# A two-block transformer kernel: convolution tables loaded instead of built, a home of its own for one tile, and another start

## The chip, the cores and the metric

The kernel runs on one core of one Trainium2 chip. The metric is the device time of one launch in microseconds (us), as the median of several runs. Beside it there is one profiled execution, with the start and duration of the instructions of each engine: TensorE (PE, matrix products; PEld is its weight load), VectorE (DVE), ScalarE (ACT), GpSimd (POOL) and SyncE (SP, which here issues nearly all transfers). Transfers are issued by an engine into its queue and then carried out by 16 DMA engines.

## The reference

The input is x of 256 tokens by 1024 features. Two hybrid layers (attention beside retention, then an MLP), an "even" mixer (block attention beside a pooling) and an "odd" mixer follow each other. Nearly everything is a product with streamed float32 weights. The change touches the beginning and the odd mixer, whose second half is a causal depthwise convolution with 31 taps:

```python
def odd_mixer(h, w_in, lam_re, lam_im, log_dt, b_re, b_im, c_re, c_im, d,
              glu_w, glu_b, dw, ln_g, ln_b, pw, w_out):
    z = h @ w_in
    su, gc, ca, cb, gd = jnp.split(z, ..., axis=-1)
    y = s5_ssm(su, lam_re, lam_im, log_dt, b_re, b_im, c_re, c_im, d)
    ya, yb = jnp.split(y @ glu_w + glu_b, 2, axis=-1)
    ssm_out = ya * jax.nn.sigmoid(yb) * jax.nn.silu(gc)
    conv_out = conformer_conv(ca, cb, dw, ln_g, ln_b, pw) * jax.nn.silu(gd)
    return jnp.concatenate([ssm_out, conv_out], axis=-1) @ w_out

def conformer_conv(a, gl, dw, ln_g, ln_b, pw):
    g = a * jax.nn.sigmoid(gl)
    c = lax.conv_general_dilated(g, kern, (1,), [(CONV_K - 1, 0)], feature_group_count=CONV_WIDTH)
    n = layer_norm(c) * ln_g + ln_b
    return jax.nn.silu(n) @ pw
```

s5_ssm is a diagonal state space recurrence over the 256 tokens.

## The kernel before

**Weights.** They come in chunks of 128 x 2048 float32 (1 MB, tile `raw`, three buffers), issued by SP in the order of use (`fetch`, L325; the first two chunks in four pieces of 128 x 512 each, L334). ACT rounds each chunk to `hi` (L336), DVE takes the rest `lo` (L337), each in halves with five buffers. PE makes three products of each pair of tiles: hi by the rounded activations, lo by them, and hi by the activations' rest (L404 to L406 in the first group `ng`, L391 to L393 in narrow ones).

**Order.** A framework of tiles and pools orders each engine's instructions by priorities when the program is built. A tile takes the place of an earlier one with the same pool and tag, once that one's last reader is done. On an engine, and in its queue, things go strictly in their order: an instruction that waits holds all behind it.

**Start.** SP issues the first piece of weights, then 8 KB of norm weights (`pv`), then the first pair of slices of x (128 x 2 x 256, 256 KB), and so on by turns; x is loaded in four such pairs (L1534). ACT scales and rounds x to `xs` (L464), DVE makes the rest (L465), and the first group of 48 products (`ng`, eight slices of 1024 features, six products each) begins.

**Odd mixer.** The projections come in the order su, cb, ca, cb, ca, gc, gd (banks `su`, `cb`, `ca`, `og`). For the convolution, the gated signal `g` (a part of the tile `big`, four groups of 128 channels) is copied by DMA into strips that hold four shifted copies: `strip(p)` issues 16 small transfers on SP (L1331) for two of the four groups, into `g4[p]`. Strip 0 lies in the place "pwc" (freed by ACT's last activation for `Q`, L1207, which follows POOL's memset of Q), strip 1 in the place "E", a table that DVE's `states(q)` reads for the last time in `wall<-wall,E` of states(3). `convolve(p)` makes 64 products of 128 x 32 weights `taps` (L1349; each float32 product is two records in the trace); POOL builds the taps from the packed filter in `pv` and small unit matrices in `ct`, into three buffers (L1338). Then PE makes `ys`, the S5 output, with `K` (L1403) and `Q` with the states `wall` (L1410), the layer mean `mu` over the convolution's result (L1390), the gated unit `gb` and `ga` and the output `yo`.

The line that matters most for the order is the place of the strips:

```python
g4[p] = s5["pool"].tile([P, 2, 4, GS + 1], F32, name="g4", tag=("pwc", "E")[p], bufs=1)
```

Of the kernel before, what the change touches and what calls it, by code (L numbers as in the profile page):

```python
# [45 lines left out]
LOWS, LOWW, LOWX = 1500, 250, 300  # L46
KP = 8
# [105 lines left out]
def pack_weights(cs, inp):  # L153
# [3 lines left out]
    for blocks, n in zip(cs, w):  # L157
# [17 lines left out]
       ("glub", 8), ("dw", 16 * KP), ("lng", 4), ("lnb", 4), ("sinks", 16)]  # L175
# [9 lines left out]
def strips(dw):  # L185

    t = np.zeros((4 * KP, 512), np.float32)
    t[:CONVK] = dw
    return t.reshape(4, KP, 4, 4, 32).transpose(0, 4, 2, 1, 3).reshape(P, 16 * KP)


def pack_vectors(inp):
    def v(a):
        return np.asarray(a, np.float32).reshape(-1, P).T

    cols = [v(inp["g_mix"]), v(inp["g_mlp"]), v(inp["g_final"]), v(inp["pre_norm_g_2"]), v(inp["post_norm_g_2"]),
            v(inp["e_pool_scale_2"]), v(inp["o_d_2"]), v(inp["o_glu_b_2"]),
            strips(inp["o_dw_2"][0]),
            v(inp["o_ln_g_2"]), v(inp["o_ln_b_2"]),
            np.broadcast_to(inp["sinks"].reshape(1, 16), (P, 16))]  # L200
    return np.ascontiguousarray(np.concatenate(cols, axis=1))
# [16 lines left out]
_CT = [("ident", 128), ("mask0", 128), ("maske", 256), ("ecos", 64), ("esin", 64), ("blk", 128), ("icnt", 64), ("e32", 32)]  # L218
# [11 lines left out]
def tables():  # L230
# [43 lines left out]
    put("e32", np.tile(np.eye(32), (4, 1)))  # L274
# [6 lines left out]
def build(ctx, tc, w, xin, pv_in, ct_in, s5_in, pg_in, out, parts=(0, 1, "e", "o"), dbg=None):  # L281
# [33 lines left out]
    def fetch(pieces=None):  # L315
# [10 lines left out]
        for h in range(0, n, HW):  # L326
# [4 lines left out]
            for c in range(0, m, step):  # L331
# [4 lines left out]
                A.copy(hi[:, s], raw[:, rs])  # L336
# [16 lines left out]
    ones = const.tile([P, P], F32, name="ones")  # L353
    V.memset(ones, 1.0)
# [256 lines left out]
    def layer(l, xh, xl, norm, after_mixer, done):  # L611
# [218 lines left out]
        after_mixer()  # L830

# [55 lines left out]
        cur = up_out(bs[0])  # L887
        for j in range(16):
# [371 lines left out]
    def odd(pool, xh, xl, n, s5, tabs5):  # L1260
# [29 lines left out]
        pg = pool.tile([P, D], F32, name="pg", tag="cd", bufs=1)  # L1290

        def states(q):
# [5 lines left out]
            tb = pool.tile([P, 2, 4 * NC], F32, name="tb", tag="tb", bufs=2)  # L1298
# [10 lines left out]
            tb = pool.tile([P, 2, 4 * NC], F32, name="tb", tag="tb", bufs=2)  # L1309
# [24 lines left out]
        def taps(q, h):  # L1334
            n = 2 * KP
            o = PVO["dw"] + (2 * q + h) * n
            tap[q, h] = pool.tile([P, n, 32], F32, name="taps", tag="taps", bufs=3)
            G.tensor_tensor(tap[q, h], pv[:, o:o + n, None].to_broadcast([P, n, 32]),  # L1338
                            C("e32")[:, None, :].to_broadcast([P, n, 32]), op=M)

        def convolve(p):
            b = bank("sm", "cq").rearrange("p (j t) -> p j t", j=2)
            for j in range(2):
                q = 2 * p + j
                for k in range(KP):
                    if k % 4 == 0:
                        taps(q, k // 4)
                    for r in range(4):
                        T.matmul(b[32 * r:32 * r + 32, j, :], tap[q, k // 4][:, 4 * (k % 4) + r, :],  # L1349
                                 g4[p][:, j, r, k:k + S], start=k == 0, stop=k == KP - 1)  # L1350
            A.copy(cv[:, 2 * p:2 * p + 2, :], b)

        for p in range(2):
# [9 lines left out]
            if p == 0:  # L1363
# [58 lines left out]
        for p, b in enumerate(t_quad("acc", "gb", ih, il)):  # L1422
            for j in range(2):
# [3 lines left out]
                stt(gc[:, n, :], th, 1.0, gc[:, n, :], AD, M)  # L1427
        gas = t_quad("acc", "ga", ih, il, hook=lambda: later.append(nv.rstd()))
# [113 lines left out]
    nc.sync.dma_start(pv[:, NG:], pv_in[:, NG:])  # L1542
# [5 lines left out]
    gg = const.tile([P, KT], F32, name="gg")  # L1548
# [114 lines left out]
```

## Time and profile before

| | |
|---|---|
| median of three runs | 1066.11 us (1065.13 to 1067.0) |
| profiled execution, its own time | 1064.91 us |
| its span, first to last instruction | 1063.1 us |
| PE busy | 1025.0 us, 96% |
| DVE, ACT, POOL busy | 759.9, 547.1, 22.7 us |
| longest idle time of PE | 17.82 us, at 972.62 |
| PE idle before its first product | 7.37 us |

The profiled execution took 1.81 us more than its span, and lies 1.20 us under the median. "Busy" of PE counts a product until its modelled end, at whichever clock it ran, so that a busy PE can still be a slow one: the first products follow each other at 0.43 us, later ones of the same form at 0.23 us.

### The profile page before, as it was taken

The numbers are of one execution on the slowest core, as the hardware profiler recorded it, in microseconds if no ns is written. First come the engines' busy times: TensorE is split into PE (matmuls) and PEld (weight loads), VectorE is DVE, ScalarE is ACT, GpSimd is POOL, SyncE is SP. The second block draws the span as 40 slices with busy tenths as digits, with TensorE's granted clock in tenths as the row PEclk, the third lists the DMA queues.
The fourth block names the chain that finished last, engine by engine and source line by source line (L and its number), as shares of the span: only waits on it lengthen the run. The fifth ranks groups of instructions, "written<-read, shape, count | busy, mean of one in ns | idle before, by whom it ended". The sixth has DMA issues, their size and how long they took to land.

```text
span 1063.1 us, 16059 instructions
## 1 busy us (share of the span) xinstructions
PE 1025.0 (96%) x6404; PEld 882.6 (83%) x6404; DVE 759.9 (71%) x1306; ACT 547.1 (51%) x844; POOL 22.7 (2%) x24
## 2 busy tenths in 40 slices
PE   7999999999999999999999999999999998995796
PEld 5887888988888888887888988888878998994595
DVE  6768656785666659478566999965677886879085
ACT  6545653554445455547544554445475557562052
POOL 0000000000000000000000000000000030012000
PEclk9999999999999999999999999999999999998799
DMA  9654445455555545544445555555545443444121
GB/s 333 227 175 154 159 138 180 163 195 196 181 198 176 198 171 186 198 158 153 153 149 193 171 194 198 176 199 179 198 153 182 151 159 121 150 139 176 35 80 40
DMA packets 29274, 179.05 MB, mean 168 GB/s; under 512 B 3600, under 2 KB 5776, under 8 KB 8592
## 3 DMA queue, kind: packets, MB, share of 16 engines
q1 hardware_dynamic: 28624, 176.44, 48.2%
q8 instruction: 50, 0.82, 0.3%
q0 software_dynamic: 288, 1.07, 0.3%
q10 hardware_dynamic: 288, 0.52, 0.1%
q14 instruction: 24, 0.20, 0.1%
HBM read 174.82 MB, written 1.05 MB: 165 GB/s over the span
## 4 chain that ended last, share of the span: by engine, by line
PE 91%; DVE 4%; ACT 2%; DMA 1%; issue 1%; SPq 1%; DVEq 0%; ACTq 0%
PE up L842 11%; PE ng L406 6%; PE ng L404 6%; PE ng L405 6%; PE up L843 6%; PE dn L865 5%; PE dn L864 5%; PE dn L866 5%; PE gate L404 3%; PE gate L406 3%; PE gate L405 3%; PE yb L406 1%; PE yb L404 1%; PE yb L405 1%; DVE lo L337 1%
## 5 line engine op out<-in xcount | busy, mean ns | idle before, releaser
L337 DVE TENSOR_TENSOR lo<-raw,hi 128x1024 fp32r<-128x1024 f32 (+1 forms) x331 | 399.1, 1210 | 188.8 <-ACT hi L336 187.2
L336 ACT CAST hi<-raw 128x1024 fp32r<-128x1024 f32 (+1 forms) x331 | 342.6, 1039 | 313.1 <-PE dn L866 81.7
L842 PE MATMUL up<-xs,hi 128*128 128x512 f32 x512 | 182.0, 398 | 0.8 <-DVE xs L465 0.8
L843 PE MATMUL up<-xs,lo 128*128 128x256 f32 x512 | 143.6, 280 | 0.0
L842 PEld LDWEIGHTS up<-xs,hi 128*128 128x128 f32 x512 | 96.2, 188 | 24.4 <-DVE xs L465 1.2
L404 PE MATMUL ng<-hi,xs 128*128 128x512 f32 x272 | 108.4, 399 | 8.2 <-ACT xs L464 8.2
L405 PE MATMUL ng<-lo,xs 128*128 128x512 f32 x272 | 107.0, 393 | 0.0
L406 PE MATMUL ng<-hi,xs 128*128 128x512 f32 x272 | 106.7, 394 | 0.1
L864 PE MATMUL dn<-hi,uph 128*128 128x512 f32 x256 | 100.1, 391 | 0.0
L865 PE MATMUL dn<-lo,uph 128*128 128x512 f32 x256 | 99.9, 390 | 0.0
L866 PE MATMUL dn<-hi,upl 128*128 128x512 f32 x256 | 99.6, 389 | 0.0
L843 PEld LDWEIGHTS up<-xs,lo 128*128 128x128 f32 x512 | 96.7, 189 | 1.0
L404 PEld LDWEIGHTS ng<-hi,xs 128*128 128x128 f32 x272 | 51.6, 190 | 18.9 <-ACT xs L464 8.7
L406 PEld LDWEIGHTS ng<-hi,xs 128*128 128x128 f32 x272 | 51.3, 189 | 11.8 <-DVE xs L465 1.0
L405 PEld LDWEIGHTS ng<-lo,xs 128*128 128x128 f32 x272 | 51.7, 190 | 10.6
L864 PEld LDWEIGHTS dn<-hi,uph 128*128 128x128 f32 x256 | 48.1, 188 | 10.5
L866 PEld LDWEIGHTS dn<-hi,upl 128*128 128x128 f32 x256 | 48.1, 188 | 10.2
L865 PEld LDWEIGHTS dn<-lo,uph 128*128 128x128 f32 x256 | 48.1, 188 | 8.9
L404 PE MATMUL gate<-hi,xs 128*128 128x512 f32 x128 | 51.6, 403 | 0.0
L406 PE MATMUL gate<-hi,xs 128*128 128x512 f32 x128 | 49.9, 390 | 0.0
L405 PE MATMUL gate<-lo,xs 128*128 128x512 f32 x128 | 49.9, 390 | 0.0
L850 ACT COPY upa<-up 128x256 f32<-128x256 f32 x64 | 23.7, 370 | 47.8 <-PE up L843 47.8
(382 smaller groups left out, 1920.5 us busy)
## 6 DMA issues: line engine op xcount, KB each, us to landing
raw<-w_dram SPq DMA_DIRECT2D x161, 1024.0 KB, 4.9
raw<-w_dram SPq DMA_DIRECT2D x9, 256.0 KB, 5.6
g<-big SPq DMA_DIRECT2D x32, 65.8 KB, 2.0
x<-x_dram SPq DMA_DIRECT2D x4, 256.0 KB, 5.7
ctm<-ct_dram SPq DMA_DIRECT2D x1, 640.0 KB, 10.1
sp<-s_dram POOLq DMA_DIRECT2D x1, 536.0 KB, 4.0
pg<-pg_dram POOLq DMA_DIRECT2D x1, 512.0 KB, 3.7
out_dram<-xn SPq DMA_DIRECT2D x2, 256.0 KB, 2.0
```

Of the source, the lines that this page charges most:

```text
L336: A.copy(hi[:, s], raw[:, rs])
L337: V.tensor_tensor(lo[:, s], raw[:, rs], hi[:, s].bitcast(F32), op=OP.subtract)
L404: T.matmul(b[t], xh[:, k, ts], hi[:, ws], start=f, stop=False)
L405: T.matmul(b[t], xh[:, k, ts], lo[:, ws], start=False, stop=False)
L406: T.matmul(b[t], xl[:, k, ts], hi[:, ws], start=False, stop=e)
L842: T.matmul(bs[i], hi[:, ws], xs2[:, k], start=k == 0, stop=False, skip_group_check=True)
L843: T.matmul(bs[i][:, 1, :], lo[:, ws], xh2[:, k, :], start=False, stop=k == KT - 1, skip_group_check=True)
L850: A.copy(u[:, j, :], b[:, 0, :])
L864: T.matmul(accs[t][h], th[:, kk, tk], hi[:, ws], start=f, stop=False)
L865: T.matmul(accs[t][h], th[:, kk, tk], lo[:, ws], start=False, stop=False)
L866: T.matmul(accs[t][h], tl[:, kk, tk], hi[:, ws], start=False, stop=e)
```

## The change

- The filter's four tables (128 x 1024 each, 512 KB) are packed outside, at the end of the array that holds `pv`, and loaded ready for use: two by POOL's queue (into the places "sp" and "cd", when these are free), the third by SP's queue and the fourth by ACT's (both into a buffer of the `xs` tag, free when the last `og` product is done). POOL's building of taps goes, and with it `dw` in `pv` and `e32` in `ct`.
- Strip 1 has a home of its own (tag "g4"). Strip 0 stays in "pwc".
- The load of `pg` (the last norm's weights) moves behind the convolution; `tb` has one buffer instead of two; `fs` is allocated later.
- Start: x goes out on ACT's queue in five pieces (slices 0, 1, 2-3, 4-5, 6-7) ahead of everything else on ACT; PE is given 11 products of `ones` with `ones` (128 x 128 float32, bank `idle`); a copy of one column makes ACT load its table then; the first piece's `hi` is made by DVE.
- `after_mixer()` (the preparation of the S5 scalars) is called a little later in the program's text; it moves no instruction on any engine.

```diff
+NIDLE = 11
...
+                if pieces is not None and i + h + c == 0:
+                    V.tensor_copy(hi[:, s], raw[:, rs])
+                else:
+                    A.copy(hi[:, s], raw[:, rs])
...
-            tb = pool.tile([P, 2, 4 * NC], F32, name="tb", tag="tb", bufs=2)
+            tb = pool.tile([P, 2, 4 * NC], F32, name="tb", tag="tb", bufs=1)
...
         def strip(p):
 
-            g4[p] = s5["pool"].tile([P, 2, 4, GS + 1], F32, name="g4", tag=("pwc", "E")[p], bufs=1)
+            n = 2 * 4 * (GS + 1)
+            if p == 0:
+                t = s5["pool"].tile([P, n], F32, name="g4", tag="pwc", bufs=1)
+            else:
+                t = pool.tile([P, n], F32, name="g4", tag="g4", bufs=1)
+            g4[p] = t.rearrange("p (j r t) -> p j r t", j=2, r=4)
...
-        def taps(q, h):
-            n = 2 * KP
-            o = PVO["dw"] + (2 * q + h) * n
-            tap[q, h] = pool.tile([P, n, 32], F32, name="taps", tag="taps", bufs=3)
-            G.tensor_tensor(tap[q, h], pv[:, o:o + n, None].to_broadcast([P, n, 32]),
-                            C("e32")[:, None, :].to_broadcast([P, n, 32]), op=M)
+        def taps():
+
+            n = KP * P
+            late = acts.tile([P, 4 * n], F32, name="taps", tag="xs", bufs=2)
+            for q in range(4):
+                if q < 2:
+                    home, tag = ((s5["pool"], "sp"), (pool, "cd"))[q]
+                    t = home.tile([P, n], F32, name="taps", tag=tag, bufs=1)
+                else:
+                    t = late[:, (q - 2) * n:(q - 1) * n]
+                (G, G, nc.sync, nc.scalar)[q].dma_start(t, pv_in[:, NPV + q * n:NPV + q * n + n])
+                tap[q] = t.rearrange("p (n c) -> p n c", c=32)
...
-                G.dma_start(pg, bass.AP(tensor=pg_in.tensor, offset=pg_in.offset, ap=[[0, P], [1, D]]))
...
+        taps()
         convolve(0)
         states(2)
         convolve(1)
         states(3)
-
-        fh, fl, fs = twin("fs")
+        pg = pool.tile([P, D], F32, name="pg", tag="cd", bufs=1)
+        G.dma_start(pg, bass.AP(tensor=pg_in.tensor, offset=pg_in.offset, ap=[[0, P], [1, D]]))
...
+    for k0, k1 in ((0, 1), (1, 2), (2, 4), (4, 6), (6, 8)):
+        nc.scalar.dma_start(x[:, k0:k1, :], xin[:, k0:k1, :])
+    idle = bank("sm", "idle")
+    for _ in range(NIDLE):
+        T.matmul(idle[:, 0:P], ones, ones, start=True, stop=True)
+    A.copy(gg[:, 0:1], ones[:, 0:1])
...
         if i in (0, 2, 4, 6):
-            p = i // 2
-            nc.sync.dma_start(x[:, 2 * p:2 * p + 2, :], xin[:, 2 * p:2 * p + 2, :])
-            split_pair(xh, xl, x, "g_mix", 0, p)
+            split_pair(xh, xl, x, "g_mix", 0, i // 2)
```

**The strips, on SP.** SP's order in the odd mixer, before (`raw` is a chunk of weights, `g<-big` a strip; the numbers behind names only tell buffers apart):

```order
L325 DMA raw_8952<-w_dram 128x2048
L325 DMA raw_9030<-w_dram 128x2048
L1331 DMA g_8660<-big 32x2x263 x16
L325 DMA raw_9093<-w_dram 128x2048
L325 DMA raw_9509<-w_dram 128x2048
L325 DMA raw_9581<-w_dram 128x2048
L325 DMA raw_9672<-w_dram 128x2048
L1331 DMA g_8857<-big 32x2x263 x16
L325 DMA raw_9729<-w_dram 128x2048
```

and after the change:

```order
L328 DMA raw_8964<-w_dram 128x2048
L1340 DMA g_8673<-big 32x2x263 x16
L1340 DMA g_8869<-big 32x2x263 x16
L328 DMA raw_9042<-w_dram 128x2048
L328 DMA raw_9105<-w_dram 128x2048
L1353 DMA taps<-pv_dram 128x1024
L328 DMA raw_9513<-w_dram 128x2048
L328 DMA raw_9586<-w_dram 128x2048
```

The second strip moved from behind four chunks to directly behind the first; one chunk (raw_9030, now raw_9042) moved from ahead of both strips to behind them, and the third table stands behind it and its successor.

On ACT, the activations that fill Q, the last of which frees strip 0's home, stand before the change as follows:

```order
L1207 ACTIVATE Q<-pwc 64x16x16 x3
L336 CAST hi_1024_8740<-raw_8734 128x1024
L1207 ACTIVATE Q<-pwc 64x16x16 x2
L336 CAST hi_0_8797<-raw_8795 128x1024
L1207 ACTIVATE Q<-pwc 64x16x16 x2
L1357 ACTIVATE cth<-cth 128x512
L1207 ACTIVATE Q<-pwc 64x16x16 x7
L336 CAST hi_1024_8801<-raw_8795 128x1024
L1207 ACTIVATE Q<-pwc 64x16x16
L336 CAST hi_0_8891<-raw_8889 128x1024
L1207 ACTIVATE Q<-pwc 64x16x16
```

and after it:

```order
L1213 ACTIVATE Q<-pwc 64x16x16 x8
L342 CAST hi_1024_8752<-raw_8746 128x1024
L1213 ACTIVATE Q<-pwc 64x16x16 x2
L342 CAST hi_0_8809<-raw_8807 128x1024
L1213 ACTIVATE Q<-pwc 64x16x16 x2
L1370 ACTIVATE cth<-cth 128x512
L1213 ACTIVATE Q<-pwc 64x16x16 x4
```

Two casts that stood between activations of Q now stand behind the last one.

**The convolution, on PE.** Before, from the last two groups of `cq` on (`ys<-uP,K` is a product of the S5 output):

```order
L1349 MATMUL cq<-g_8660,taps 32x256 x64
L1349 MATMUL cq<-g_8857,taps 32x256 x2
L1403 MATMUL ys<-uP,K 128x256
L1349 MATMUL cq<-g_8857,taps 32x256
L1403 MATMUL ys<-uP,K 128x192
L1349 MATMUL cq<-g_8857,taps 32x256 x61
L1403 MATMUL ys<-uP,K 128x128
```

and after:

```order
L1362 MATMUL cq<-g_8673,taps 32x256 x64
L1362 MATMUL cq<-g_8869,taps 32x256 x64
L1417 MATMUL ys<-uP,K 128x256
L1417 MATMUL ys<-uP,K 128x192
L1417 MATMUL ys<-uP,K 128x128
```

The second convolution's products stand together, and all products of `ys` behind them; their number is the same.

**The start, on ACT.** Before:

```order
L336 ACT_TABLE_LOAD
L336 CAST hi_0_81<-raw_80 128x512
L464 ACTIVATE xs<-x,pv 128x256 x2
L336 CAST hi_0_81<-raw_80 128x512
L336 CAST hi_1024_95<-raw_80 128x512
L464 ACTIVATE xs<-x,pv 128x256 x2
L336 CAST hi_1024_95<-raw_80 128x512
```

and after:

```order
L1545 DMA x<-x_dram 128x256 x2
L1545 DMA x<-x_dram 128x512 x3
L1549 ACT_TABLE_LOAD
L1549 COPY gg<-ones 128x1
L471 ACTIVATE xs<-x,pv 128x256 x2
L342 CAST hi_0_100<-raw_99 128x512
L471 ACTIVATE xs<-x,pv 128x256 x2
L342 CAST hi_1024_113<-raw_99 128x512 x2
```

Five issues of x stand ahead of the table load, and the first `xs` directly behind it and the one-column copy. The fifth issue waits for a semaphore that the 8 KB `pv` transfer on SP also counts on.

## Rows read from the trace of the kernel before

**Rows 1.** The page's part 4: the chain that ended last, by engine.

```profile
PE 91%; DVE 4%; ACT 2%; DMA 1%; issue 1%; SPq 1%; DVEq 0%; ACTq 0%
```

**Rows 2.** PE's timeline in the odd mixer: start, duration, instruction, idle before.

```profile
965.48 7.14 PE L1349 MATMUL cq<-g,taps 128*32 128x256 f32 x128
990.44 1.69 PE L1349 MATMUL cq<-g,taps 128*32 128x256 f32 x4 [17.82 <-DMA g<-big]
...
1005.78 2.62 PE L1403 MATMUL ys<-uP,K 128*128 128x256 f32 x16
1008.33 1.97 PE L1410 MATMUL ys<-wall,Q 128*32 128x63 f32 x128
1010.23 1.99 PE L1390 MATMUL mu<-big,ones 128*128 128x256 f32 x8
```

**Rows 3.** SP's timeline in the odd mixer, same columns.

```profile
945.40 12.64 SPq L1331 DMA_DIRECT2D g<-big  x16
958.15 10.75 SPq L325 DMA_DIRECT2D raw<-w_dram  x4
980.62 10.18 SPq L1331 DMA_DIRECT2D g<-big  x16
```

**Rows 4.** DVE's timeline: the last reader of E.

```profile
979.90 0.69 DVE L1042 TENSOR_TENSOR wall<-wall,E 128x512 f32<-128x512 f32 x1
```

**Rows 5.** Timelines of POOL and ACT where strip 0's home comes free.

```profile
931.61 0.60 POOL L1367 DMA_DIRECT2D pg<-pg_dram  x1 [31.60 <-PE vb L1286]
```

```profile
937.10 1.06 ACT L336 CAST hi<-raw 128x1024 fp32r<-128x1024 f32 x1
...
944.90 0.42 ACT L1207 ACTIVATE Q<-pwc 64x256 f32<-64x256 f32 x1
```

**Rows 6.** Transfers of the span: KB each, us from issue to landing.

```profile
raw<-w_dram SPq DMA_DIRECT2D x161, 1024.0 KB, 4.9
...
g<-big SPq DMA_DIRECT2D x32, 65.8 KB, 2.0
x<-x_dram SPq DMA_DIRECT2D x4, 256.0 KB, 5.7
...
pg<-pg_dram POOLq DMA_DIRECT2D x1, 512.0 KB, 3.7
...
pv<-pv_dram SPq DMA_DIRECT2D x1, 8.0 KB, 2.8
```

**Rows 7.** Busy time by stretch: length, engines (instructions), granted clock, DMA share, GB/s.

```profile
3.00:6.00 3.00, 0.00 (x0) 0.00 (x0) 0.69 (x1) 0.62 (x1) 0.00 (x0) 1.00 0.84 154
...
12.00:15.00 3.00, 3.00 (x15) 2.47 (x14) 3.00 (x8) 3.00 (x8) 0.00 (x0) 1.00 1.02 417
...
894.00:896.00 2.00, 2.00 (x70) 1.78 (x72) 0.30 (x1) 1.13 (x3) 0.00 (x0) 0.52 0.00 0
...
973.00:990.00 17.00, 0.00 (x0) 0.00 (x0) 8.28 (x14) 0.28 (x1) 1.87 (x1) 0.64 0.22 52
```

**Rows 8.** The timeline of all engines at the start.

```profile
0.74 1.28 ACT L336 ACT_TABLE_LOAD   x1 [0.74 <-PEq L1653]
...
1.19 0.42 SPq L1531 DMA_DIRECT2D pv<-pv_dram  x1
1.65 0.43 SPq L1534 DMA_DIRECT2D x<-x_dram  x1
...
6.81 0.91 ACT L464 ACTIVATE xs<-x,pv 128x256 fp32r<-128x256 f32 x2 [2.38 <-DMA x<-x_dram]
...
7.37 0.79 PE L404 MATMUL ng<-hi,xs 128*128 128x512 f32 x1 [7.37 <-ACT xs L464]
...
11.80 0.43 PE L405 MATMUL ng<-lo,xs 128*128 128x512 f32 x1
...
20.25 0.39 PE L406 MATMUL ng<-hi,xs 128*128 128x512 f32 x1
```

**Rows 9.** PE's timeline: two float32 products of 128 x 128 (four records).

```profile
894.19 1.06 PE L543 MATMUL rb<-ct,ny 128*128 128x128 f32 x4
```

More of the change, by code (lines that the diff above doesn't have):

```diff
@@ L174 @@
 _PV = [("g_mix", 16), ("g_mlp", 16), ("g_final", 8), ("pre", 16), ("post", 16), ("pscale", 4), ("d", 4),
-       ("glub", 8), ("dw", 16 * KP), ("lng", 4), ("lnb", 4), ("sinks", 16)]
+       ("glub", 8), ("lng", 4), ("lnb", 4), ("sinks", 16)]
 PVO = {}
@@ L188, in strips @@
     t[:CONVK] = dw
-    return t.reshape(4, KP, 4, 4, 32).transpose(0, 4, 2, 1, 3).reshape(P, 16 * KP)
+    t = t.reshape(4, KP, 4, 4, 32).transpose(0, 2, 1, 3, 4)
+    z = np.zeros((4, 32, 4, KP, 4, 32), np.float32)
+    for c in range(32):
+        z[:, c, ..., c] = t[..., c]
+    return z.reshape(P, 512 * KP)
 def pack_vectors(inp):
@@ L197, in pack_vectors @@
             v(inp["e_pool_scale_2"]), v(inp["o_d_2"]), v(inp["o_glu_b_2"]),
-            strips(inp["o_dw_2"][0]),
             v(inp["o_ln_g_2"]), v(inp["o_ln_b_2"]),
-            np.broadcast_to(inp["sinks"].reshape(1, 16), (P, 16))]
+            np.broadcast_to(inp["sinks"].reshape(1, 16), (P, 16)), strips(inp["o_dw_2"][0])]
     return np.ascontiguousarray(np.concatenate(cols, axis=1))
@@ L215, in pack_s5 @@
     return np.ascontiguousarray(np.concatenate(cols, axis=1))
-_CT = [("ident", 128), ("mask0", 128), ("maske", 256), ("ecos", 64), ("esin", 64), ("blk", 128), ("icnt", 64), ("e32", 32)]
+_CT = [("ident", 128), ("mask0", 128), ("maske", 256), ("ecos", 64), ("esin", 64), ("blk", 128), ("icnt", 64)]
 _MT = [("rcos", 256), ("rsin", 128), ("acos", 128), ("asin", 64), ("mask1", 256), ("dm", 1024)]
@@ L273, in tables @@
     put("blk", blk)
-    put("e32", np.tile(np.eye(32), (4, 1)))
     return t
@@ L335, in fetch @@
                     pieces((h + c) // 512)
-                A.copy(hi[:, s], raw[:, rs])
+                if pieces is not None and i + h + c == 0:
+                    V.tensor_copy(hi[:, s], raw[:, rs])
+                else:
+                    A.copy(hi[:, s], raw[:, rs])
                 V.tensor_tensor(lo[:, s], raw[:, rs], hi[:, s].bitcast(F32), op=OP.subtract)
@@ L353, in build @@
     ones = const.tile([P, P], F32, name="ones")
+    gg = const.tile([P, KT], F32, name="gg")
     V.memset(ones, 1.0)
@@ L829, in layer @@
         dump(f"xa{l}", x)
-        after_mixer()
         def up(j, hook=None):
@@ L887, in layer @@
         cur = up_out(bs[0])
+        after_mixer()
         for j in range(16):
@@ L1288, in inputs @@
                 vbs.append(vb)
-        pg = pool.tile([P, D], F32, name="pg", tag="cd", bufs=1)
         def states(q):
@@ L1308, in states @@
                 V.tensor_tensor_scan(wt[:, a], mf, wt[:, a], 0.0, M, AD)
-            tb = pool.tile([P, 2, 4 * NC], F32, name="tb", tag="tb", bufs=2)
+            tb = pool.tile([P, 2, 4 * NC], F32, name="tb", tag="tb", bufs=1)
             tt(tb, wt, es, M)
@@ L1345, in convolve @@
                 for k in range(KP):
-                    if k % 4 == 0:
-                        taps(q, k // 4)
                     for r in range(4):
-                        T.matmul(b[32 * r:32 * r + 32, j, :], tap[q, k // 4][:, 4 * (k % 4) + r, :],
+                        T.matmul(b[32 * r:32 * r + 32, j, :], tap[q][:, 4 * k + r, :],
                                  g4[p][:, j, r, k:k + S], start=k == 0, stop=k == KP - 1)
@@ L1427, in odd @@
                 stt(gc[:, n, :], th, 1.0, gc[:, n, :], AD, M)
+        fh, fl, fs = twin("fs")
         gas = t_quad("acc", "ga", ih, il, hook=lambda: later.append(nv.rstd()))
@@ L1541, in build @@
     fetch()
-    nc.sync.dma_start(pv[:, NG:], pv_in[:, NG:])
+    nc.sync.dma_start(pv[:, NG:], pv_in[:, NG:NPV])
     nr = CTO["mask1"][0] - NCC
```

1 line of the change is left out of this document (removed).

## The prediction

> **What bounds the kernel now.** I read the chain first: PE carries 91% of it [rows 1], and PE is busy for 1025.0 of the span's 1063.1 us. A change gains here only where PE waits or where its products run slowly. So I read PE's timeline next, and there are two such places.
>
> In the odd mixer the first convolution's 64 products (128 records) start at 965.48 and take 7.14; then PE stands still for 17.82 us, until 990.44, for strip 1's transfer [rows 2]. SP's timeline says why that is so late: its sixteen issues take 10.18 us from 980.62 on, while the four chunks ahead of them were issued by 968.9 [rows 3]. DVE's timeline shows what they waited for: the last reader of E, strip 1's home, runs from 979.90 to 980.59 [rows 4]. Behind the stop PE first works slowly: the granted clock in it was 0.64, and four records took 1.69 us where 128 had taken 7.14 [rows 7, 2].
>
> At the start PE has its first product at 7.37, released by ACT's `xs`, which waited for x until 6.81 although x was issued at 1.65 [rows 8]. The first ten steps from product to product take 4.43 us together (7.37 to 11.80), the next 37 take 8.45 (to 20.25), which is 0.443 and 0.228 us each [rows 8]. [...]
>
> Everything after both places is PE back to back, so that what is gained there stays gained up to the end.
>
> **Part 1: the odd mixer.** From the end of the first convolution (965.48 + 7.14 = 972.62) to the start of `mu` (1010.23) PE now needs 37.61 us [rows 2]. After the change the same stretch holds a wait w, the second convolution in one piece, and `ys` in two rounds of 16 records with K and 128 with Q. With the durations from start to start, 7.14 for the convolution, 2.55 (1005.78 to 1008.33) for K and 1.90 (1008.33 to 1010.23) for Q [rows 2], that is 7.14 + 2 x (2.55 + 1.90) = 16.0 us. The gain is 37.61 - 16.0 - w = 21.6 - w.
>
> The wait w ends with the last of strip 1, table 2 and table 3. Strip 1 first. Its home is new, so it waits only for g, and stands directly behind strip 0. Strip 0 waits for ACT's last activation of Q, which ended at 945.32 (944.90 + 0.42) [rows 5]. Two casts of 1.06 us leave the row ahead of it on ACT, and 0.60 us of POOL's issue of `pg` ahead of Q's memset goes [rows 5]. That would put Q's end at 942.6, if no cast that stays waits longer; I take 943.5, and keep 945.4 as its bound. Sixteen issues took 10.18 us undisturbed, 12.64 with a chunk still landing beside them [rows 3]. Two strips are then 20.4 to 22.8 us: issued by 963.9 from 943.5, landed 2.0 later [rows 6] at 965.9. By itself strip 1 is no wait at all.
>
> Table 2 stands on SP behind both strips and two chunks, and its place comes free with the last `og` product at about 965.5, where the first convolution starts. A chunk of 1024 KB lands 4.9 us after its issue [rows 6], so the first lands at 968.8; the second, at the 417 GB/s that the queues reach [rows 7], 2.5 us later at 971.3; tables 2 and 3 are together another 1024 KB and are there at 973.8. I take 974.0, so w = 974.0 - 972.6 = 1.4. The bounds: with strips that start at 945.4 and take 21.3 both chunks go out at 966.7, and the tables land at 966.7 + 4.9 + 2.5 + 2.5 = 976.6, so w = 4.0; from below, a table alone would be there 3.7 us after 965.5 [rows 6], ahead of 972.6, and w = 0. The gain of this part is **20.2 us, between 17.6 and 21.6**.
>
> What is late next? `ys` needs the states of states(3) on DVE, whose operation on E ended at 980.59 before [rows 4]. DVE's order now has the rests of both chunks behind the strips ahead of the last state operations; the second chunk is there at 971.3, ACT's two casts of 1.06 us [rows 5] take it to 974, and behind them DVE has two rests of 128 x 1024 and four state operations, which I estimate at 5 us from the 0.69 of one of 128 x 512 [rows 4]: about 980. PE comes to these states at 974.0 + 7.14 + 2.55 + 1.90 + 2.55 = 988.1. The cover is 8 us. The chunks for `gb`, formerly issued before the strips, land by 971.3 for a use at about 991. Cost zero; if they came 10 us later, PE would wait for them instead.
>
> Tables 0 and 1 go on POOL's queue: table 0 when "sp" is free, table 1 behind Q's memsets, which end before the first activation of Q, 937 at the latest [rows 5]. A 512 KB load on this queue took 3.7 us [rows 6], and the first convolution wants them at 965: covered by over 25 us. POOL's issue costs 0.60, and neither lies ahead of Q's memsets. `pg` goes out late, at about 975, and is wanted behind the last products, at 1055: covered. `tb` with one buffer is written and read by DVE alone, in order: zero. The taps' building on POOL goes; nobody but the convolution waited for it. The later `after_mixer()` moves no instruction: zero.
>
> **Part 2: the start.** ACT now issues five transfers first. At 0.43 each [rows 8] four end at about 2.5; the fifth waits for `pv`, issued at 1.19 and landed 2.8 later [rows 8, 6], at 4.0, or at 5.0 if x beside it slows it. Then 0.43 for the issue, 1.28 for the table load [rows 8], an estimated 0.2 for the copy of one column: the first `xs` begins at 5.9 to 6.9 instead of 6.81. PE's eleven products end before or about then: two of the same form took 1.00 us at the lower clock (894.19 to 895.19, granted 0.52) [rows 9, 7], so eleven take at most 5.5, from 1.1 to 6.6. PE's first real product comes at 6.5 to 7.5; I take 7.0, a gain of 0.4, bounds -0.1 and 0.9.
>
> The larger part is the clock. PE rose to its faster pace 4.43 us after its first product [rows 8]. With eleven products from 1.1 on, the same would end near 5.6, ahead of the first real one; the ten slow steps then take 10 x 0.228 instead of 4.43, a gain of 2.15, between 0 and 2.2. Can weights and x keep up? A slice needs 128 KB of x and 256 KB of weights, 384 KB in 6 x 0.228 = 1.37 us, at 417 GB/s 0.94 us [rows 7]; ACT needs half of 0.91 and half of 1.06, 1.0 us a slice [rows 8, 5]. But between 3 and 6 us only 154 GB/s flowed [rows 7], and the second to fourth slices may be late by some tenths; I take off 0.25. This part is worth **2.3 us, between -0.2 and 3.0**.
>
> [...]
>
> **The sum.** 20.2 + 2.3 = 22.5 us off the profiled execution's 1064.91 makes 1042.4. The median lies 1.2 above that execution (1066.11), so I forecast **1043.6 us**.
>
> **Rivals.**
> *The start gives nothing* (chance 0.15): ACT reaches `xs` as late as now, and PE, idle between its eleven products and the first real one, is slow again, or it waits for slices. Against it: the gap would be some 1 us by the reckoning above, and over the 17 us of the stop in the odd mixer the granted clock was still 0.64 in the mean, between its two levels [rows 7]. Time: 1066.1 - 20.2 = 1045.9.
>
> *Table 2 is late behind the chunks* (0.20). The price is set by SP's order: the table stands behind 2 MB of weights which nobody needs so soon. For it speaks that strip 0's sixteen issues took 12.64 and not 10.18 [rows 3], and that the rate beside small strip pieces may be under 417. With landing at 976.6 to 978, w is 4.0 to 5.4: 1046.2 to 1047.6.
>
> *Strip 1 still waits for an old reader* (0.03), the case on the slower side. If its home came free no sooner than E does, at 980.6, its issues would end at 990.8 [rows 3], the two chunks and table 2 would follow, which stood ahead of it or did not exist before, and the tables would land 9.9 later (4.9 + 2.5 + 2.5) at 1000.7. Then `mu` starts at 1000.7 + 16.0 = 1016.7, 6.5 later than now; less 2.3 from the start that is 1070.3. It decides from a second convolution later than 1010.2 + 2.3 - 16.0 = 996.5 on. Against it: the new home has no earlier tenant in the order, and the strip waits only for g.
>
> *A smaller gain of some other cause* (0.06): 1049 to 1056, such as states or weights of `gb` that come 10 us later than reckoned.
>
> **How the numbers follow.** The forecast has the remaining 0.56, with 1042 to 1045.5 as its own range. Low end: both parts at their best, 21.6 + 3.0, give 1041.5, and I go to 1041. High end: table late and start without gain, 17.6 and 0, give 1048.5; 1049. Within this lie about 85%. About 0.2%, 2.1 us, is what a measurement of this kernel can tell from no change: faster 0.95, same 0.02, slower 0.03.
>
> **What would show it.** In the changed kernel's trace: SP issues 32 strip transfers in a row from 943 to 945.4 on, without the stop to 980.6; PE's idle time ahead of the second convolution is 0 to 4 us instead of 17.8 and released by a table; its products follow at full pace; `mu` starts about 16 us after that convolution. At the start: eleven idle products, the first `ng` near 7.0, and steps of 0.23 from the first on. Wrong would be: a wait for `wall` in `ys`, a wait for weights in `gb`, steps of 0.43 at the start, or idle time of PE between the slices of the first group.

## The result, and the profile after

The changed kernel took 1049.91 us in the median (1048.1 to 1053.7, four runs) against 1066.55 us before: a ratio of 0.9849, 95% interval 0.9817 to 0.9881. It is faster by 16.6 us where 22.9 were forecast, and lies 0.9 us above the range's upper end. The profiled execution took 1051.13 us with a span of 1049.3, that is 13.8 less span than before; the working below is for this execution, whose gain is smaller than that of the medians.

The page of the changed kernel, parts 1 and 4:

```profile
PE 1027.2 (98%) x6426; PEld 889.4 (85%) x6426; DVE 756.6 (72%) x1307; ACT 546.3 (52%) x844; POOL 11.0 (1%) x18
...
PE 90%; DVE 3%; DMA 3%; ACT 2%; SPq 2%; issue 1%; ACTq 0%; DVEq 0%
```

PE is busier, yet DMA and SP's queue have a larger share of the chain than in [rows 1]. PE's waits in the changed kernel (engine, line, what it waited for; sum, times, longest) name five places:

```profile
PE cq L1362 <- DMA taps<-pv_dram: 4.1, 1, 4.1
PE su L400 <- issue: 2.0, 1, 2.0
PE ng L411 <- ACT xs L471: 1.6, 3, 0.8
PE kb L1243 <- issue: 1.3, 1, 1.3
PE ng L411 <- ACT hi L342: 1.2, 1, 1.2
...
PE ss L511 <- DVE sqf L487: 0.7, 1, 0.7
```

The 17.8 us for strip 1 are gone. In their place stands a wait of 4.1 for a table, and there are waits that the kernel before did not have: for weights in the first group (1.2), for statistics in the second (0.7), and 2.0 us at `su` for nothing that the profile shows as a wait.

**The odd mixer after.** PE's and SP's timelines answer to [rows 2] and [rows 3]:

```profile
967.16 7.14 PE L1362 MATMUL cq<-g,taps 128*32 128x256 f32 x128
978.41 9.11 PE L1362 MATMUL cq<-g,taps 128*32 128x256 f32 x128 [4.11 <-DMA taps<-pv_dram]
987.45 2.62 PE L1417 MATMUL ys<-uP,K 128*128 128x256 f32 x16
990.00 1.97 PE L1424 MATMUL ys<-wall,Q 128*32 128x63 f32 x128
991.90 2.62 PE L1417 MATMUL ys<-uP,K 128*128 128x256 f32 x16
994.44 1.97 PE L1424 MATMUL ys<-wall,Q 128*32 128x63 f32 x128
996.34 2.00 PE L1404 MATMUL mu<-big,ones 128*128 128x256 f32 x8
```

```profile
943.94 22.85 SPq L1340 DMA_DIRECT2D g<-big  x32
966.89 1.02 SPq L328 DMA_DIRECT2D raw<-w_dram  x2
968.01 0.38 SPq L1353 DMA_DIRECT2D taps<-pv_dram  x1
```

Both strips go out in one piece, as forecast. From the first convolution to `mu` PE needs 29.18 us (967.16 to 996.34) where it needed 44.75 (965.48 to 1010.23): a gain of 15.57. The two things that are larger than forecast are the wait of 4.11 and the second convolution, 9.11 instead of 7.14. Busy time by stretch (columns as in [rows 7]) shows why the convolution is slow:

```profile
974.30:978.40 4.10, 0.00 (x0) 0.00 (x0) 4.07 (x6) 2.13 (x4) 0.53 (x1) 1.00 1.01 419
978.40:980.00 1.60, 1.59 (x25) 1.59 (x29) 1.60 (x3) 0.70 (x1) 0.00 (x0) 0.88 0.98 387
980.00:982.00 2.00, 2.00 (x26) 1.96 (x20) 1.97 (x4) 0.12 (x1) 0.00 (x0) 0.50 1.02 381
982.00:984.00 2.00, 2.00 (x33) 1.98 (x29) 1.19 (x2) 0.92 (x1) 0.00 (x0) 0.74 1.03 395
```

The granted clock is still 1.00 while PE stands idle; it falls to 0.50 only when PE is at work again, and is back at 1.00 from 984 to 986. In the same four rows the DMA engines are full, at 381 to 419 GB/s: first the two chunks, which nobody needs yet, and the tables, then a third chunk and `pg`. The full DMA engines are not what makes the convolution slow: in `fill` below they are as full (share 1.02) beside the first 67 records of it, and the granted clock stays at 1.00.

**The start after.** PE's timeline, answering to [rows 8]:

```profile
1.06 5.06 PE L1548 MATMUL idle<-ones 128*128 128x128 f32 x22 [1.06 <-DVE ones L361]
6.88 0.50 PE L411 MATMUL ng<-hi,xs 128*128 128x512 f32 x1 [0.76 <-ACT xs L471]
...
8.14 0.39 PE L413 MATMUL ng<-hi,xs 128*128 128x512 f32 x1
9.71 0.50 PE L411 MATMUL ng<-hi,xs 128*128 128x512 f32 x1 [1.17 <-ACT hi L342]
```

The eleven products do what they should: the first real one comes at 6.88 and the steps are at 0.23 us from the second one on. ACT's timeline shows what held its table load behind the issues of x:

```profile
4.93 1.28 ACT L1549 ACT_TABLE_LOAD   x1 [4.93 <-DMA x<-x_dram]
```

The fifth issue of x went out at 4.57, when x's first piece had landed (4.55) and the 8 KB of `pv` had not (4.71). So it waited for x, and not for a semaphore of `pv`, as the text ahead of the prediction and the prediction have it; that the time fell between 4.0 and 5.0, as forecast, is luck.

But the second slice has no weights until 9.71: its piece was issued at 1.65 and landed at 9.02. And the chain of waits in the same execution (start, duration, what) shows a second loss, at the statistics:

```profile
2.14 8.42 DMA x<-x_dram
...
10.58 6.59 DMA raw<-w_dram
...
17.20 1.06 ACT hi L342
...
18.29 1.22 DVE lo L343
19.51 0.60 DVE sqacc L502
20.11 1.14 DVE lo L343
21.25 0.61 DVE sqacc L502
...
21.89 0.43 DVE sqf L487
...
22.36 0.61 PE ss L511 x4
```

It begins with a transfer of x that landed only at 10.56. SP's third chunk of weights waits for that landing (0.5 us; SP's pieces ahead of it had already waited 3.6 us for x in two places, though x goes out on ACT), is issued at 10.58 where it was 8.90 before, and its casts and rests stand on ACT and DVE ahead of the sums of squares; `ss` on PE, in the middle of the second group, waits for those until 22.36. In the kernel before it ran at 20.48 without a wait.

### The profile page after: what moved, and what is told of

Its sections match the earlier page's. It is cut to its first block, busy times and chain, and to the rows that moved or that the text cites. A ratio compares the mean times of both kernels' runs of the same rounds, so it can differ in the third digit from the quotient of the medians.

```text
span 1049.3 us, 16091 instructions
## 1 busy us (share of the span) xinstructions
PE 1027.2 (98%) x6426; PEld 889.4 (85%) x6426; DVE 756.6 (72%) x1307; ACT 546.3 (52%) x844; POOL 11.0 (1%) x18
## 4 chain that ended last, share of the span: by engine, by line
PE 90%; DVE 3%; DMA 3%; ACT 2%; SPq 2%; issue 1%; ACTq 0%; DVEq 0%
PE up L847 11%; PE up L848 6%; PE ng L413 6%; PE dn L869 6%; PE dn L870 6%; PE dn L871 5%; PE ng L412 5%; PE ng L411 5%; PE gate L411 3%; PE gate L413 3%; PE gate L412 3%; SPq L1340 1%; PE yb L413 1%; PE yb L412 1%; PE yb L411 1%; DVE lo L343 1%
## 5 line engine op out<-in xcount | busy, mean ns | idle before, releaser
L411 PEld LDWEIGHTS ng<-hi,xs 128*128 128x128 f32 x272 | 51.1, 188 | 13.9 <-ACT xs L471 2.4
```

The costliest lines, as they stand in the source:

```text
L411: T.matmul(b[t], xh[:, k, ts], hi[:, ws], start=f, stop=False)
```

## The experiments

Twelve more runs were made, the first of them the changed kernel again. All times are medians, each ratio is to the kernel before in its own batch (there at 1065.16 to 1066.55 us), and the marks are from each kernel's profiled execution: start of the 1st and 48th product of the first group, of the first product of `up`, PE's stops that the profile calls "issue" (no wait is shown) before `su` ends, PE's wait before the second convolution and that convolution's duration.

| kernel | us | ratio (95%) | 1st, 48th | `up` | issue stops | wait, 2nd conv. |
|---|---|---|---|---|---|---|
| before | 1066.55 | 1 | 7.37, 20.25 | 215.56 | kb 1.6 | 17.82 |
| changed | 1049.91 | 0.9849 (0.9817-0.9881) | 6.88, 19.45 | 215.70 | kb 1.3, su 2.0 | 4.11, 9.11 |
| after_again | 1050.52 | 0.9864 (0.9848-0.9879) | 6.81, 19.59 | 216.85 | kb 0.3, su 1.75 | 3.81, 7.42 |
| start_old | 1050.20 | 0.9853 (0.9839-0.9868) | 7.21, 20.39 | 215.70 | kb 1.5 | 4.14, 9.76 |
| start_sp | 1051.33 | 0.9866 (0.9845-0.9886) | 7.11, 18.22 | 215.73 | kb 0.4, su 1.75 | 3.22, 7.45 |
| start_pair | 1048.35 | 0.9846 (0.9832-0.9859) | 6.47, 17.33 | 213.49 | kb 1.0, su 1.75 | 3.76, 9.11 |
| tab_first | 1045.47 | 0.9811 (0.9797-0.9825) | 6.70, 18.32 | 215.26 | kb 1.7, su 1.75 | none, 7.1 |
| fill | 1047.02 | 0.9828 (0.9814-0.9841) | 6.62, 17.67 | 213.73 | kb 0.2, su 2.0 | none, stop of 1.7 inside |
| home_e | 1064.16 | 0.9984 (0.9975-0.9993) | 6.62, 18.51 | 215.06 | kb 2.1, su 1.75 | 15.23 |
| pool_taps | 1045.74 | 0.9818 (0.9805-0.9832) | 6.74, 19.01 | 216.23 | kb 0.2, su 1.7 | none, 7.1 |
| idle0 | 1050.96 | 0.9855 (0.9831-0.9878) | 7.04, 20.48 | 216.87 | kb 2.0 | 3.08, 9.07 |
| idle_wide | 1047.69 | 0.9831 (0.9809-0.9853) | 6.56, 19.46 | 217.00 | kb 0.7 | 3.42, 9.11 |
| pair_tab | 1044.82 | 0.9799 (0.9781-0.9817) | 6.68, 17.58 | 213.69 | kb 1.1, su 2.3 | none, 7.1 |
| pair_tab_wide | 1042.09 | 0.9779 (0.9764-0.9795) | 6.30, 19.02 | 216.43 | kb 1.7 | none, 7.1 |

The profiled executions differ in three stretches only: up to `up`, from the first product of `bt` (887 in the kernel before) through `kb` and `su` to the first of `cb`, and from the first convolution to `mu`. From `up` to `bt` they agree within 0.6 us, from `cb` to the first convolution within 0.02, and from `mu` to the end within 0.7.

**The changed kernel again.**

> The changed kernel once more, as the base for the runs beside it. Its four runs so far lay between 1048.1 and 1053.7 us, the two odd places of its trace being a wait of 4.1 us for a table with a second convolution of 9.1 instead of 7.1 us behind it, and 2.0 us without a cause at the first products of su. If these two recur in every execution, the time is again 1048 to 1054; if the 2.0 us are a chance of one execution, they are absent in this trace and the lower end, 1048, is the rule.

The wait recurs (3.81) and so does the stop at `su` (1.75). The second convolution took 7.42 this time, and the mean granted clock of the profiled execution was 0.997 where it had been 0.994, so the clock does not fall in every execution: of the seven traces with this wait the convolution was slow (9.07 to 9.76) in five, behind waits of 3.08 to 4.14, and fast in two, behind 3.22 and 3.81. That alone makes some 2 us of spread between executions.

**The home alone.** Strip 1 back in the place "E":

```diff
-            if p == 0:
-                t = s5["pool"].tile([P, n], F32, name="g4", tag="pwc", bufs=1)
-            else:
-                t = pool.tile([P, n], F32, name="g4", tag="g4", bufs=1)
+            t = s5["pool"].tile([P, n], F32, name="g4", tag=("pwc", "E")[p], bufs=1)
```

> Strip 1 goes back to the home E, all else as in the changed kernel, tables by DMA included. Theory A: the home alone brought the gain in the odd mixer; SP waits for the last reader of E again, issues strip 1 from about 980 on, the second convolution starts near 990 and the time is that of the kernel before, 1064 to 1068. Rival: the loaded tables bring part of it (POOL's building held DVE up, and with it the last reader of E): then strip 1 is issued 3 us or more sooner and the time is 1060 to 1063.

SP's and DVE's timelines of this kernel:

```profile
978.30 10.18 SPq L1337 DMA_DIRECT2D g<-big  x16
```

```profile
970.00 0.69 DVE L929 SCALAR_TENSOR_TENSOR big<-big,gu 128x512 f32<-128x512 f32 x1
...
977.58 0.69 DVE L1048 TENSOR_TENSOR wall<-wall,E 128x512 f32<-128x512 f32 x1
```

Nearly all of the gain goes with the home; it is the one that counts. The rival has a small part of the truth: DVE reaches E's last reader at 977.58 instead of 979.90 [rows 4], strip 1 goes out 2.3 us sooner, and 1.5 us remain (0.9984, clear of 1). In the kernel before, the same DVE operations were slower while POOL built taps (967.55 to 974.86): 1.54 us instead of 0.69 for one of 128 x 512, 2.92 instead of 1.27 for a pair of scans. DVE's order differs in the two kernels as well, so that this share of the 2.3 us is not shown by itself.

**The table's place.** The third table with a higher priority, which puts it one strip transfer ahead of the chunks:

```diff
+TAPHI = 600
...
+                with tc.high_priority(TAPHI if q == 2 else 0):
-                (G, G, nc.sync, nc.scalar)[q].dma_start(t, pv_in[:, NPV + q * n:NPV + q * n + n])
+                    (G, G, nc.sync, nc.scalar)[q].dma_start(t, pv_in[:, NPV + q * n:NPV + q * n + n])
```

> The third table's transfer stands on SP directly ahead of the last transfer of strip 1, and so ahead of the two chunks, instead of behind them; nothing else is moved. Theory A (the wait before the second convolution is the table's place behind 2 MB of weights, and the slow stretch in it is the wait's consequence): the wait falls to under 1 us, the second convolution takes 7.1 us, and the time is 5 to 6 us below the changed kernel. Rival (the DMA engines are busy with the chunks whatever the order, or the fourth table on ACT ends last at 975.9): a wait of 1.5 to 3 us remains, 2 to 4 us below.

PE's timeline there, and the transfers of both kernels between 960 and 985 (KB each, us to landing), first with the table ahead, then in the changed kernel:

```profile
965.69 14.05 PE L1364 MATMUL cq<-g,taps 128*32 128x256 f32 x256
979.67 2.62 PE L1419 MATMUL ys<-uP,K 128*128 128x256 f32 x16
```

```profile
taps<-pv_dram SPq DMA_DIRECT2D x1, 512.0 KB, 5.1
taps<-pv_dram ACTq DMA_DIRECT2D x1, 512.0 KB, 5.3
```

```profile
taps<-pv_dram ACTq DMA_DIRECT2D x1, 512.0 KB, 8.6
taps<-pv_dram SPq DMA_DIRECT2D x1, 512.0 KB, 10.4
```

All 256 records run without a stop or a slow stretch, and the time falls by 5.1 us (1050.52 to 1045.47). Theory A holds: the wait was the place behind 2 MB of weights, and the slow stretch came with the wait: it stands in five of the seven traces that have the wait and in none of the five that have none. Nothing waited for the chunks, which now came later.

**Work instead of the wait.** The first half of `ys` between the two convolutions, `outputs` being the body of the loop that makes it:

```diff
         convolve(0)
         states(2)
+        y0 = outputs(0)
         convolve(1)
```

> The first half of ys (16 records with K, 128 with Q) stands on PE between the two convolutions instead of behind them; the transfers are as in the changed kernel. Theory A: these 4.45 us of work fill the wait of 4.1 us, the clock doesn't fall, and the time is 5 to 6 us below the changed kernel. Rival: the second convolution is slow for a reason of its own (its operands, its place beside the transfers), then it takes 9 us again and the time is 4 us below.

```profile
975.45 4.05 PE L1362 MATMUL cq<-g,taps 128*32 128x256 f32 x67
981.22 3.67 PE L1362 MATMUL cq<-g,taps 128*32 128x256 f32 x61 [1.72 <-issue]
```

There is no wait for the table and no slow stretch, as theory A says, but PE stopped for 1.72 us in the middle of the convolution, again for what the profile calls "issue" (the last section says what stands beside such stops); 3.5 us were gained, not 5 to 6.

**POOL's building in the new homes.** The four loads replaced by POOL's products of before, with their packed filter and unit matrices:

```diff
-                (G, G, nc.sync, nc.scalar)[q].dma_start(t, pv_in[:, NPV + q * n:NPV + q * n + n])
                 tap[q] = t.rearrange("p (n c) -> p n c", c=32)
+                for h in range(2):
+                    m = 2 * KP
+                    o = PVO["dw"] + (2 * q + h) * m
+                    G.tensor_tensor(tap[q][:, m * h:m * h + m, :], pv[:, o:o + m, None].to_broadcast([P, m, 32]),
+                                    C("e32")[:, None, :].to_broadcast([P, m, 32]), op=M)
```

> POOL builds the tables again, as before the change, into the changed kernel's four places; strip 1 keeps its own home; no table is loaded. Theory A (the wait is the transfer's queue): the last two tables are built in four steps of 1.9 us from 966.7 on, just ahead of the second convolution, whose wait is under 1 us; the time is 4 to 6 us below the changed kernel. Rival: POOL's building slows DVE (a 128 x 512 operation took 1.54 instead of 0.68 beside it), so that the states or the weights' rests come late and ys waits: less than 3 us below, or above it.

Theory A again: 1045.74, 4.8 us under the changed kernel and equal to the table ahead of the chunks. POOL's building delayed nobody that matters. So the loading of the tables, placed as it was, made this kernel slower than building them in the same places would have been; with the third table ahead of the chunks the two are equal.

**The start undone.** All of the start as before, the rest as changed:

> The whole start as in the kernel before (x on SP by turns with the weights, no products of ones, the first cast and the table load on ACT), all else as in the changed kernel. Theory A: the start as a whole is worth nothing, because what the clock gives is lost to weights that come later; then this kernel takes the same time as the changed one within 0.7 us. Theory B, the forecast: the start is worth 2.3 us; then it is 2.3 us slower.

1050.20 against 1050.52: theory A for the time, the whole start is worth nothing. The first `up` comes at 215.70 with the old start, and at 215.70 and 216.85 in the two executions of the changed kernel; behind it, the old start has no stop at `su`, which the new one pays with 1.75 to 2.0 us.

**x back on SP, and only the first pair on ACT.** In start_sp every pair of x goes out on SP by turns again; in start_pair the first two slices stay on ACT:

```diff
-    for k0, k1 in ((0, 1), (1, 2), (2, 4), (4, 6), (6, 8)):
+    for k0, k1 in ((0, 1), (1, 2)):
         nc.scalar.dma_start(x[:, k0:k1, :], xin[:, k0:k1, :])
...
-            split_pair(xh, xl, x, "g_mix", 0, i // 2)
+            p = i // 2
+            if p:
+                nc.sync.dma_start(x[:, 2 * p:2 * p + 2, :], xin[:, 2 * p:2 * p + 2, :])
+            split_pair(xh, xl, x, "g_mix", 0, p)
```

> Only the transfers of x go back to SP, by turns with the weights in four pairs; the eleven products, the early table load and the cast on DVE stay. Theory A (x on its own queue took the bandwidth from the second piece of weights, which PE waited 1.17 us for): the first product comes at about 7.3, the first 48 end by 18.5 and not 19.8, and the time is 1 to 2.3 us below the changed kernel. Rival: the statistics' chain (sums of squares) on ACT and DVE sets the end of the first group whatever the weights do; then the time is that of the changed kernel within 0.7 us.

> Only the first pair of slices of x goes out on ACT (two pieces of 128 KB), the other three pairs on SP by turns with the weights; products of ones, early table load and cast on DVE stay. Theory A: the weights are late by 256 KB at most, and ACT is not held by a fifth transfer, so that the first product comes at 5.5 to 6.7 and the time is 1.5 to 3 us below the changed kernel. Rival (the statistics' chain): within 0.7 us of it.

With x on SP the 48th product comes at 18.22, 2.0 us sooner than before, as theory A wanted; then PE stops for 1.4 us, this time for a rest of the third chunk, and `up` comes no sooner (215.73). The time is that of the changed kernel (0.8 us above its second measurement, well within the spread): the expectation of theory A for the whole was a miss. With the first pair on ACT the gain outlives the group in the profiled execution (`up` at 213.49), and the median is 2.2 us below the changed kernel, with intervals that overlap. Neither the weights nor the statistics alone set the start: in the changed kernel PE waits for the second piece and for the statistics, in start_sp for the third chunk's rest, and what is late next takes the gain.

What sets `up` is in the traces: the waits that PE has between its first slice and 28 us. In the six executions with the changed kernel's start they add up to 0.50 (`fill`), 1.13 (`home_e`), 1.29 (`tab_first`), 1.89 (`changed`), 2.17 (`pool_taps`) and 2.80 us (`after_again`), and `up` comes at 213.73, 215.06, 215.26, 215.70, 216.23 and 216.85, in the same order. They are waits for the second piece of weights, for rests and for the statistics. That piece was issued at 1.65 in all six and landed between 6.95 and 9.18; why its landing differs so much is not shown.

**The products of ones.** Left out, and then made wider:

```diff
-    for _ in range(NIDLE):
-        T.matmul(idle[:, 0:P], ones, ones, start=True, stop=True)
+    for w4_ in (4, 4, 2):
+        T.matmul(idle[:, 0:w4_ * P], ones, ones[:, None, :].to_broadcast([P, w4_, P]), start=True, stop=True)
```

> The changed kernel without its eleven products of ones; x on ACT, table load and cast on DVE stay. Theory A (PE's stops without a cause at su, 1.75 to 2.03 us in every trace with the eleven products and in neither without, are PE waiting for its own instructions, 16 KB at a time, and the 44 more instructions at the start shift where a block ends): the stop at su is gone and one of about 1.5 us stands at kb, as before the change. The first products run at 0.43 us again. The two nearly cancel: the time is that of the changed kernel within 1 us. Rival (the stop at su comes from the later x or the smaller tables): it is there again, and the time is 1 to 2 us above.

> The eleven products of 128 x 128 become two of 128 x 512 and one of 128 x 256, about as long but 32 fewer instructions in PE's stream, weight loads counted. Theory A (instruction blocks): PE's stops at kb and su change their sizes or places, in the sum about 1.5 to 2 us as before the change, and the time is 0 to 1.5 us below the changed kernel. Rival: su stops for 1.7 to 2.0 us as it does with eleven.

The stop at `su` stands in all nine traces with eleven products and in none of the five without them (before, start_old, idle0, idle_wide, pair_tab_wide). PE's waits in idle0 and in idle_wide:

```profile
PE kb L1243 <- issue: 2.0, 1, 2.0
```

```profile
PE kb L1243 <- issue: 0.7, 1, 0.7
```

For the stops that is theory A in both, though in idle_wide 0.7 us remain and not 1.5 to 2. idle0 takes the time of the changed kernel, as it said, but partly by chance: from `bt` to `cb` it needs 18.73 us where the changed kernel needs 18.78, because its stop at `kb` is longer (2.0) and the granted clock fell behind it, to 0.55 and 0.60 in 900 to 904. idle_wide takes 2.8 us less than the changed kernel's second measurement, which is more than theory A said, with intervals that just meet (0.9853 and 0.9848).

**Together.**

> Two experiments together: the third table ahead of the chunks, and only the first pair of x on ACT's queue. Theory A: SP's third chunk no longer waits for the landing of x's later pieces, so that the first group's statistics come in time, and the table's wait is gone; the two gains (5 us and 1 to 2 us) add up to 6 to 7 us below the changed kernel, 1043.5. Rival: the start's gain is lost again in a wait further on, and the time is that of the table alone, 1045.5.

> As the run before it, with two products of 128 x 512 and one of 128 x 256 in place of the eleven. Theory A (instruction blocks): below it by up to 1.5 us, 1042 to 1043.5. Rival: the same as with eleven products.

The third table first and the first pair of x on ACT: 1044.82 us, 5.7 below the changed kernel's second measurement and not 6 to 7. The pair of x adds 0.7 to the table alone, which is not clear of the spread, so the rival, 1045.5, is the nearer. Its trace shows the rival's loss: `up` comes 1.6 us sooner than in tab_first (213.69), but from `bt` to `cb` PE needs 20.41 us instead of 17.66.

With three wide products in place of the eleven it is 1042.09 us, in theory A's range, 8.4 below the changed kernel's second measurement and 23 below the kernel before. The two medians differ by 2.7 us, with intervals that overlap, and the stop is not the whole of it. Busy time by stretch, first with eleven products, then with three:

```profile
890.00:892.00 2.00, 2.00 (x11) 2.00 (x10) 0.96 (x6) 1.17 (x2) 0.00 (x0) 0.50 0.63 258
...
900.00:902.00 2.00, 2.00 (x11) 2.00 (x11) 1.77 (x5) 0.00 (x0) 0.00 (x0) 0.50 0.03 8
```

```profile
890.00:892.00 2.00, 1.35 (x12) 1.35 (x12) 1.08 (x1) 2.00 (x5) 0.00 (x0) 1.00 0.78 256
...
900.00:902.00 2.00, 2.00 (x18) 1.94 (x17) 2.00 (x6) 0.26 (x1) 0.00 (x0) 1.00 0.00 0
```

From `bt` to `cb` the kernel with three needs 4.58 us less: the stop at `su` (2.3) is gone, and so are two stretches at half clock, 2.9 us together; the stop at `kb` is 0.6 longer. The second of these stretches stands behind the stop at `su`, as one does in start_pair; the first stands ahead of both stops, in most traces and in the kernel before (0.52 from 894 to 896 [rows 7]), and what decides it is not shown. Against this the start lost 2.74 us (`up` at 216.43), and the wide products did not give it its pace this time:

```profile
6.30 0.79 PE L412 MATMUL ng<-hi,xs 128*128 128x512 f32 x1 [0.61 <-ACT xs L472]
6.89 0.63 PE L413 MATMUL ng<-lo,xs 128*128 128x512 f32 x1
```

The steps are at 0.43 up to 10.30, as without any products of ones; in idle_wide, with the same three, they were at 0.23. One execution of each does not show why.

## Why the prediction was wrong

Right were the main mechanism, and the view that carried it: the new home lets strip 1 go out behind strip 0, PE's 37.61 us from the end of the first convolution to `mu` shrink to w + 16.0 and what the slow convolution adds, and the states and the weights of `gb` are never late. home_e shows that this is the home and not the tables. Of the forecast 22.5 us in the profiled execution 13.9 came, to the start of `mu`:

- **The wait w** was put at 1.4 us and measured 4.11, just over its bound of 4.0. Two terms were mis-sized. The strips were issued by 966.8 and not 963.9: they began at 943.94, nearly as taken (943.5), but 32 issues took 22.85 us and not 20.4, which was twice the figure of sixteen undisturbed ones; 22.8 stood in the text as the other end. And the way from the chunks' issue to the table took 11.5 us (966.9 to 978.4) instead of 9.9. The rival "table 2 is late behind the chunks" had the price and the place: 4.0 to 5.4. I gave it 0.20; both of its rows, [rows 3] and the order of SP, spoke for it, and the value should have been taken from there.
- **The second convolution** was put at 7.14 and took 9.11. I asked what the clock does at the start and did not ask it of the new wait, though the first place of the very same argument was that PE is slow behind a stop. That is 1.97 us, a term that the sum put at nothing; in tab_first, without the wait, it takes 7.1.
- **The start** was put at 2.3 and was worth -0.14 up to `up`, and nothing in the medians. The step that failed is "can weights and x keep up?". It priced x's bytes (a slice in 0.94 us) but not what x on a queue of its own costs the weights: their second piece came at 9.0; and it did not follow SP's queue, where the third chunk waits for x's landing and the statistics hang on that chunk. The prediction's own sign of being wrong, idle time of PE between the slices of the first group, came with 1.17 us. The pace was right in itself: ten steps at 0.23 instead of 0.44. That it is the clock is read from the pace alone, for the granted clock reads 1.00 in the kernel before as well, from 7 to 12 us, where the steps are at 0.43:

```profile
9.00:10.00 1.00, 1.00 (x4) 0.81 (x3) 1.00 (x3) 1.00 (x3) 0.00 (x0) 1.00 1.05 346
```

- **The stop at `su`**, 2.02 us beside one of 1.34 at `kb` (before: 1.58 at `kb` alone), was in no part of the sum. I costed the eleven products as time at the start, and not as instructions in PE's stream. The step that failed is "Everything after both places is PE back to back": the kernel before already had the stop at `kb` and a granted clock of 0.52 there [rows 7]. Up to `su` 0.5 us were gained; behind its stop PE was 1.7 us late.

In numbers: 15.57 in the odd mixer instead of 20.2; -1.68 before it instead of +2.3; 13.9 together. With x on ACT's queue, transfers of 256 KB of weights took 6.8 us to land in the first 13 us where they had taken 5.7, so what x gained the weights lost. The range failed because its high end added two bad cases (late table, no start) and had no room for the slow convolution and the stop at `su`, some 2 us each. That it failed by 0.9 us only is partly luck: the changed kernel's profiled execution lies 1.2 us above its median, and that of the kernel before 1.6 below (1064.91 against 1066.55).

What stays open: in the profiled executions the very same start brought `up` at 213.73 to 216.85. The waits that make the difference are named above; why the same transfers land up to 2.2 us apart is not shown.

## What to carry to other kernels

When a wait is removed, price the next wait with the slow clock behind it (here 1.97 us), and look in the order at what stands ahead of the new last arrival in its queue: half a megabyte that is wanted now should not stand behind two that are wanted in 20 us. Price a transfer that moves to another engine's queue in the queue that it left as well: with x on ACT, 256 KB of weights on SP took 6.8 us to land instead of 5.7, and SP's third chunk waited for x and went out at 10.58 instead of 8.90. Instructions added early to a long unrolled stream were not free later on: with 44 of them at the start came the stop of 1.7 to 2.3 us at `su`, near 900. Count them, here in blocks of 256, and look at the stops called "issue" in places where the engine runs through very short instructions. What such a change is worth can differ by 2 us from one execution to the next.

## What the runs showed of the hardware

PE's stops of 0.2 to 2.3 us that the profile calls "issue" stand in or just behind stretches of very short instructions (`kb`, 32 columns each; `ys` with Q, 63 columns; `cq`), and move when the number of instructions ahead of them changes. Beside each stands a transfer of the kind "instruction". The transfers of the changed kernel from 898 to 902 (0.1 us a slice) are one only, at 898.9, with the stop at `su` from 899.57 to 901.59:

```profile
GB/s 0 0 0 0 0 0 0 0 0 164 0 0 0 0 0 0 0 0 0 0 0 0 0 0 0 0 0 0 0 0 0 0 0 0 0 0 0 0 0 0
...
## 3 DMA queue, kind: packets, MB, share of 16 engines
q8 instruction: 1, 0.02, 2.1%
```

Each of these transfers has 16 KB (50 of them on q8 in the changed kernel, 0.82 MB), and those beside the stops take 0.9 to 1.4 us; all 27 stops of over 0.15 us in the fourteen traces ended 1.2 to 1.5 us after the end of such a one. Their places go with the number of instructions. If PE's recorded instructions, products, weight loads and semaphore instructions together, are counted from the first on, 9921 or 9922 stand ahead of the stop at `kb` in every trace, 10177 ahead of the one at `su`, 11970 ahead of the one in fill's `cq`, and 12225 ahead of those in `ys` (tab_first, pool_taps, pair_tab). All these numbers leave 193 or 194 when divided by 256, whatever the instruction is, and with or without the 44 instructions at the start (why it is this remainder is not shown): the stops stand whole blocks of 256 instructions apart. About as many come to one transfer: the changed kernel has 6426 products and 6426 weight loads to its 50 transfers on q8, 257 to one. That PE waits at the block ends for its next instructions, and that a block end costs a stop where the instructions ahead of it are short, is my reading of these numbers; no record names the wait, and it was not tested by itself.

The second thing is that the granted clock fell after a stop of PE of only 3.1 to 4.1 us, when PE was at work again, and not in every execution: behind waits of 3.22 and 3.81 us it stayed up (its mean over the profiled execution was 0.997 in both), behind 3.08, 3.42, 3.76, 4.11 and 4.14 it fell (0.992 to 0.995), for 1.9 to 2.6 us of lost time. It also fell behind shorter stops: behind those at `su` of 1.75 us in start_pair and 2.3 in pair_tab, for some 1.5 us, and not behind the seven others at `su`.
